# TensorE's order inside attention written out by hand, with one filler matmul between transpositions

## The chip, the cores and the metric

The program runs on one core of a Trainium2 chip, in one launch. The metric is the device time of one execution in microseconds; a comparison of two kernels is made on the same chip, in rounds. All figures of this document are microseconds unless they are marked ns.

## The reference

The reference computes two blocks, one behind the other, on 512 positions of width 1024 (and 256 context positions in the second block). Everything is float32. Cut to what matters here:

```python
# block 1
h = rmsnorm(x) * (1 + scale1) + shift1
qa, ka, va, qb, kb, vb, ga, gb = split(h @ w_in)
ya = mixture_of_dilations(qa, ka, va)      # 8 heads of 64: softmax(q k^T + bias + mask) v
yb = neighbourhood_attention_2d(qb, kb, vb) # 8 heads of 64, window 8 x 16 on a grid of 64 columns
x += gate1 * ((sigmoid(ga) * (ya @ w_a) + sigmoid(gb) * (yb @ w_b)) @ w_out)
x += gate2 * (conv-gated feed forward of x)
# block 2, two layers; every layer has three attentions over latent and context positions
for l in range(2):
    y0 = mla(...)    # 8 heads, q and k of 96 columns, v of 128, dense
    y1 = diff(...)   # 8 heads, p0 - lambda * p1 of two score maps, v of 128, dense
    y2 = swa(...)    # 16 query heads, 4 key heads of 64, window 128 plus the context, with a sink
    x += gate * ((sum_r sigmoid(gm_r) * ((y_r * silu(z_r)) @ w_branch[r])) @ w_out)
```

## The kernel before

**Numbers.** Every product is made in float32r: an operand is held as a high part and a rest, and a projection runs three matmuls for one (`mm3`, lines 336 to 340). A projection of 128 columns over 1024 inputs and 512 positions (`proj`, line 342) is 8 x 3 matmuls of 512 columns, and 8 x 3 of 256 more where the context is projected too. `v_natural` (line 357) and `v_wide` (line 1124) make the values in 256-column matmuls.

**Attention.** Five phases follow each other in the program: the dilated and the neighbourhood attention of block 1, then MLA, diff and SWA, these three twice (layer 0 with context queries, layer 1 without). Each calls `attend` (line 420) with a list of heads; a head has a preparation (its projections, called the mandatory work) and units. A unit is two blocks of 128 queries of one head, and has two halves. `scores` makes the score matmuls (lines 1159 to 1174; into up to three PSUM banks `s`) and the softmax on VectorE and ScalarE. `values` (line 627) transposes the probabilities in groups of up to four 128x128 blocks into one PSUM bank `t` (line 647), splits each group by a ScalarE copy into `pth` and a VectorE subtraction into `ptl` (lines 381 and 382, called from line 651), and multiplies the parts with the values into the bank `pv` (line 665). The pool has one bank for `t` (line 291), two or three buffers each for `pth` and `ptl`.

**Units by phase.** A unit over latent queries has 12 transpositions in three groups of four in MLA and diff (16 and 16 such units over the two layers, each), 9 in groups of 4, 4 and 1 in SWA (32 and 32), 8 in two groups in the dilated attention (16), 5 in groups of 4 and 1 in the neighbourhood attention (16). A unit over context queries has one group of four. That is 1680 transpositions. Score matmuls of a latent unit: MLA 6 of 512 and 6 of 256 columns; diff two maps of 4 of 512 and 4 of 256 each; SWA 6 of 256 and 2 of 384; dilated 4 of 512; neighbourhood 2 of 256 and 2 of 384.

**Filler.** TensorE gets projections between the steps of a unit: `fill` (line 405) draws steps from queues of generators until a number of ns is used up. The queues are the mandatory work of the next head and `opt`, the gate projections that belong to no head. A step of `proj` is three matmuls.

**Order.** `attend` emits, for each unit, the first two groups of transpositions of the unit before, the scores of this one, filler, the first value matmuls, the third group, and so on. This is only the order in which the program is traced. The compiler's list scheduler orders the instructions of each engine anew, by its own times, and may draw ahead whatever it takes to be ready.

**Late work.** `self.late` holds generators that are stepped behind a unit (diff's normalization: `tok_sum`, line 541, writes the bank `t`, and line 558 reads it).

Of the kernel before, what the change touches and what calls it, by code (L numbers as in the profile page):

```python
# [18 lines left out]
P = 128  # L19
# [3 lines left out]
KD = D // P  # L23
# [255 lines left out]
class Prog:  # L279
    def __init__(self, tc, A, out, stage=None):  # L280
        self.tc, self.nc, self.A, self.out, self.stage = tc, tc.nc, A, out, stage
        self.n = 0
        off, self.U = 0, {}
        for name, w, _ in _units():
            self.U[name] = (off, w)
            off += w * P
        self.lay, self.nvec = _vec_layout()
        self.bg, self.ahead, self.late = [], {}, []
        self.wide, self.turn = False, 0
        self.cur = None  # L290
        self.banks = dict(mm=3, t=1, pv=1, s=3)
        self.lo = self.nc.vector
        self.spare = 0


# [39 lines left out]

    def mm3(self, ps, wh, wl, xh, xl, first, last):
        mm = self.nc.tensor.matmul
        mm(ps, wh, xh, start=first, stop=False)  # L338
        mm(ps, wl, xh, start=False, stop=False)  # L339
        mm(ps, wh, xl, start=False, stop=last)  # L340

    def proj(self, name, x, evac, kn=KD, m=P, ctx=False, k0=0, off=0, back=False, ranges=None):

        wt = self.w(name) if isinstance(name, str) else name
        for c0, n in ranges or ((0, S), (S, C))[:2 if ctx else 1][::-1 if back else 1]:
            ps = self.ps("mm")[:m, :n]
            cs = slice(c0, c0 + n)
            for k in range(kn):
                wh, wl = wt.cols(off + k * m, m)
                xh, xl = x[k0 + k] if isinstance(x[k0 + k], tuple) else (x[k0 + k][:, 0], x[k0 + k][:, 1])  # L350
                self.mm3(ps, wh, wl, xh[:, cs], xl[:, cs], k == 0, k == kn - 1)
                if k < kn - 1:
                    yield 3 * n * 0.424
            evac(ps, cs)
            yield 3 * n * 0.424

# [48 lines left out]
    def fill(self, ns, *queues):  # L405


        while ns > 0:
            if self.cur is None:
                q = next((q for q in queues if q and (not isinstance(q[0], tuple) or q[0][0]())), None)  # L410
                if q is None:
                    return
                g = q.pop(0)
                self.cur = g[1] if isinstance(g, tuple) else g
            try:
                ns -= next(self.cur)
            except StopIteration:
                self.cur = None

    def attend(self, heads, opt, opt_ns):  # L420


        nu = sum(len(h[2]) for h in heads)
        pend = None
        for i, (_, _, units) in enumerate(heads):
            mand = heads[i + 1][0]() if i + 1 < len(heads) else []
            mns = heads[i + 1][1] if i + 1 < len(heads) else 0
            for s_, v_ in units:

                vals = pend() if pend else iter(())  # L430
                next(vals, None)
                s_()
                left = mns / len(units) + opt_ns / nu
                ns = left * 0.5
                self.fill(ns, mand, opt)
                for _ in vals:
                    left -= ns
                    self.fill(min(ns, left), mand, opt)
                pend = v_
                self.fill(left - ns, mand, opt)  # L440
                self.tick(1)
                late, self.late = self.late, []
                for g in late:
                    if next(g, 0) is None:
                        self.late.append(g)
            self.finish(mand)
        for _ in pend():
            self.fill(2000, opt)
        while self.late:
            self.late = [g for g in self.late if next(g, 0) is None]  # L450
            self.fill(4000, opt)

    def finish(self, queue):

        while queue:
            self.fill(1, queue)
        self.fill(1e9)

# [168 lines left out]
    def values(self, pv, pp, chunks, stat):  # L627
# [25 lines left out]

        for grp in grps[:2]:
            turn(grp)
        yield
        for i, grp in enumerate(grps):
# [9 lines left out]
            if i + 2 < len(grps):  # L667
                turn(grps[i + 2])
            if i < len(grps) - 1:
                yield  # L670

# [94 lines left out]
    def neighbours(self, h, opt, opt_ns):  # L766

        nc = self.nc
# [6 lines left out]
        def prep(hd):  # L775
# [21 lines left out]
            def ev_v(ps, cs):  # L797
                vt = self.st()
                nc.scalar.activation(own(vt), fwd(ps), AF.Copy)
                for c in range(2):  # L800
                    tp = self.ps("t")
                    for i in range(2):
                        nc.tensor.transpose(tp[:, i * P:i * P + P], vt[:, (2 * c + i) * P:(2 * c + i) * P + P], self.ident)
                    self.v_pairs(va[c], tp[:, :256])

# [51 lines left out]
    def mixer1(self):  # L857
# [5 lines left out]
        with ExitStack() as es:  # L863
# [79 lines left out]
            y = []  # L943
            for f in (lambda: self.dilated(h, line, opt, 42000), lambda: self.neighbours(h, opt, 42000)):
                for yy in f():
# [42 lines left out]
    def ffn(self, x, xq, rbs, h, xd, x_close):  # L988
# [4 lines left out]
        with ExitStack() as es:  # L993
# [21 lines left out]
            def by_halves(nm, ev):  # L1015

                wt, ps = self.w(nm), self.ps("mm")
                for i, (c0, n_) in enumerate(HALVES):
                    cs = slice(c0, c0 + n_)
                    for k in range(KD):  # L1020
                        self.mm3(ps[:, cs], *wt.cols(k * P, P), h[k][:, 0, cs], h[k][:, 1, cs], i == 0 and k == 0,
                                 i == 1 and k == KD - 1)
                        yield 1
# [247 lines left out]
    def mla(self, l, h, ctx):  # L1271
# [60 lines left out]
        def prep(j):  # L1332
            g, e = j // 2, j % 2
            gens = []
            if e == 0:
# [3 lines left out]
                gens.append(self.proj(f"uk{l}_{g}", kvn, ev_k, kn=2, ctx=True))  # L1339
                st["v", g] = [self.page() for _ in range(2)]  # L1340
                gens.append(self.v_wide(f"ux{l}_{g}", kvn, st["v", g], 2))
            q = st["q", j] = self.page()
            ys.append(self.f3())

            def ev_q(ps, cs):
                a = self.st()[:, :ps.shape[-1]]
                if cs.start == 0:
# [4 lines left out]

            gens.append(self.proj(f"uq{l}_{j}", qn, ev_q, kn=3, ctx=ctx))
            if e:

                nc.gpsimd.tensor_copy(kt[1][64:], krp[64:])
            return gens

        def unit(j, q0, lt):
# [11 lines left out]
            def values():  # L1371
# [4 lines left out]
                if q0 in (256, S):  # L1376
# [6 lines left out]

        heads = [(lambda j=j: prep(j), (8900 if j % 2 else 8900), [unit(j, *q) for q in self.qpairs(ctx)])
                 for j in range(KD)]
        self.run_pairs(heads[0][0]())
        yield
# [37 lines left out]
    def diff(self, l, h, ctx):  # L1425
# [33 lines left out]
        def unit(j, q0, lt):  # L1459
# [287 lines left out]
```

## Time and profile before

| | us |
|---|---|
| median of 3 runs | 3565.99 (3561.65 to 3569.0) |
| the profiled execution | 3569.2 |
| its span | 3567.4 |
| TensorE busy | 3436.9 (96%) |
| TensorE's weight loads busy | 2936.5 (82%) |
| VectorE busy | 2352.8 (66%) |
| ScalarE busy | 1808.6 (51%) |

A matmul's record is longer than its place in the stream, since matmuls are pipelined: neighbouring records overlap. What one costs is read from the distance of two starts in the timeline, not from its mean duration. The granted clock is 0.99 over the span. The attention phases lie, from the span's start, at about 84 to 377 (block 1), 963 to 1246 (MLA, layer 0), 1330 to 1826 (diff), 1856 to 2262 (SWA), 2483 to 2690, 2718 to 3150 and 3190 to 3476 (the same three in layer 1).

### The profile page before, as it was taken

The page shows a single profiled execution, that of the slowest core. Times are in us where ns is not written, and L with a number is a line of the kernel's source. Part 1 is how long each engine was busy: PE and PEld are TensorE (multiplying, and loading weights), DVE is VectorE, ACT ScalarE, POOL GpSimd, SP SyncE. Part 2 cuts the span into 40 slices and gives each one's busy share as a digit, 9 for nine tenths or more (in the row PEclk, how much of TensorE's full clock was granted, in tenths as well). Part 3 has the DMA queues.
Part 4 walks back from the last instruction along what each step waited for, and adds up shares of the span by engine and source line. Part 5 has one row for each costly group of instructions (what it writes and reads, how often), then busy time and mean ns, then how long its engine had stood idle before and what let it go on. Part 6 is the DMA issues. An engine that isn't in the chain of part 4 may idle for free. (4 is left out here: it accounts for less than half of the span.)

```text
span 3567.4 us, 54501 instructions
## 1 busy us (share of the span) xinstructions
PE 3436.9 (96%) x19696; PEld 2936.5 (82%) x19696; DVE 2352.8 (66%) x4957; ACT 1808.6 (51%) x4162; POOL 450.2 (13%) x320
## 2 busy tenths in 40 slices
PE   6999999998999999999999999999999999999998
PEld 4777778776888898889888888888888888887777
DVE  7867678876445446567745677655564666757885
ACT  3456444422456525445535777425673454537772
POOL 3001046643000100001100001000010001000010
PEclk9999999998999999999999999999999999999999
DMA  6844545564221153323243211433115333262224
GB/s 227 258 155 120 156 151 161 167 206 133 77 60 35 45 156 85 95 67 85 59 147 106 60 50 47 131 106 90 60 49 149 110 92 92 79 177 80 64 69 142
DMA packets 200351, 392.41 MB, mean 110 GB/s; under 512 B 26289, under 2 KB 39857, under 8 KB 200082
## 3 DMA queue, kind: packets, MB, share of 16 engines
q1 hardware_dynamic: 199378, 385.23, 35.9%
q0 software_dynamic: 704, 3.70, 0.3%
q8 instruction: 155, 2.54, 0.3%
q14 instruction: 114, 0.93, 0.1%
HBM read 302.82 MB, written 38.83 MB: 96 GB/s over the span
## 5 line engine op out<-in xcount | busy, mean ns | idle before, releaser
L338 PE MATMUL mm<-h,whi 128*128 128x512 f32 (+2 forms) x2764 | 1001.9, 363 | 4.7 <-ACT h L601 4.1
L339 PE MATMUL mm<-h,wlo 128*128 128x512 f32 (+2 forms) x2764 | 999.3, 362 | 5.7 <-POOL wlo L275 2.9
L340 PE MATMUL mm<-h,whi 128*128 128x512 f32 (+2 forms) x2764 | 997.0, 361 | 0.1
L274 ACT ACTIVATE whi<-wraw 128x512 fp32r<-128x512 f32 (+1 forms) x763 | 470.5, 622 | 570.1 <-PE mm L340 333.3
L275 DVE TENSOR_TENSOR wlo<-wraw,whi 128x512 fp32r<-128x512 f32 (+1 forms) x627 | 440.8, 708 | 306.7 <-ACT whi L274 302.2
L339 PEld LDWEIGHTS mm<-h,wlo 128*128 128x128 f32 (+1 forms) x2764 | 526.1, 190 | 70.6 <-POOL wlo L275 4.0
L338 PEld LDWEIGHTS mm<-h,whi 128*128 128x128 f32 (+1 forms) x2764 | 526.1, 190 | 69.5 <-ACT h L601 5.0
L340 PEld LDWEIGHTS mm<-h,whi 128*128 128x128 f32 (+1 forms) x2764 | 526.0, 190 | 67.3 <-DVE h L602 0.3
L382 DVE TENSOR_TENSOR ptl<-t,pth 128x512 fp32r<-128x512 f32 (+1 forms) x480 | 298.0, 621 | 160.9 <-ACT pth L381 156.4
L381 ACT ACTIVATE pth<-t 128x512 fp32r<-128x512 f32 (+1 forms) x480 | 260.3, 542 | 221.9 <-PE t L647 217.8
L647 PE MATMUL t<-ident,p 128*128 128x128 f32 x1680 | 287.5, 280 | 30.1 <-DVE ptl L382 19.8
L647 PEld LDWEIGHTS t<-ident,p 128*128 128x128 f32 x1680 | 195.4, 141 | 96.6 <-DVE ptl L382 43.9
L275 POOL TENSOR_TENSOR wlo<-wraw,whi 128x512 fp32r<-128x512 f32 (+1 forms) x136 | 223.2, 1658 | 271.2 <-ACT whi L274 171.1
L338 PE MATMUL mm<-hl,whi 128*128 128x512 f32 (+1 forms) x680 | 242.1, 356 | 6.3 <-ACT hl L381 5.3
L339 PE MATMUL mm<-hl,wlo 128*128 128x512 f32 (+1 forms) x680 | 240.4, 354 | 0.0
L665 PE MATMUL pv<-pth,hl 128*128 128x256 f32 (+1 forms) x1184 | 224.4, 292 | 6.0 <-ACT pth L381 4.7
L1403 POOL TENSOR_TENSOR st<-st,tab 128x512 f32<-128x512 f32 x52 | 76.0, 1462 | 1197.4 <-DMA st<-st 854.0
L665 PEld LDWEIGHTS pv<-pth,hl 128*128 128x128 f32 x1184 | 178.8, 190 | 48.7 <-ACT pth L381 34.2
L1231 POOL TENSOR_TENSOR f<-f,st 128x512 f32<-128x512 f32 x72 | 86.3, 1199 | 784.0 <-DVE st L1230 608.5
L340 PE MATMUL mm<-f,whi 128*128 128x512 f32 (+1 forms) x504 | 178.0, 355 | 0.0
L1199 ACT ACTIVATE p<-s,m 128x512 f32<-128x512 f32 x192 | 132.1, 688 | 90.5 <-DVE m L1194 88.7
L665 PE MATMUL pv<-ptl,hl 128*128 128x256 f32 (+1 forms) x768 | 169.3, 295 | 1.6 <-DVE ptl L382 1.5
(265 smaller groups left out, 6369.7 us busy)
## 6 DMA issues: line engine op xcount, KB each, us to landing
wraw<-in_wst SPq DMA_DIRECT2D x734, 256.0 KB, 2.7
mraw<-in_w_mod SPq DMA_DIRECT2D x48, 512.0 KB, 4.1
hl<-hl SPq DMA_DIRECT2D x128, 192.0 KB, 3.0
mraw<-in_w_ada SPq DMA_DIRECT2D x36, 512.0 KB, 4.6
tg<-st SPq DMA_DIRECT2D x64, 256.0 KB, 2.0
st<-st SPq DMA_DIRECT2D x208, 64.0 KB, 2.0
p<-tg SPq DMA_DIRECT2D x40, 256.0 KB, 2.9
p<-tg SPq DMA_DIRECT2D x24, 384.0 KB, 3.7
```

What stands on the lines that cost most here:

```text
L274: nc.scalar.activation(hi[:, :n], raw[:, :n], AF.Copy)
L275: p.lo.tensor_tensor(lo[:, :n], raw[:, :n], hi[:, :n].bitcast(F32), op=ALU.subtract)
L338: mm(ps, wh, xh, start=first, stop=False)
L339: mm(ps, wl, xh, start=False, stop=False)
L340: mm(ps, wh, xl, start=False, stop=last)
L381: nc.scalar.activation(dst_h, src, AF.Copy)
L382: nc.vector.tensor_tensor(dst_l, src, dst_h.bitcast(F32), op=ALU.subtract)
L647: self.nc.tensor.transpose(tp[:, o + i * P:o + i * P + P], pp[t][:, cols[i]:cols[i] + P], self.ident)
L665: mm(dst, sv, x_[:, o:o + w], start=first, stop=last)
L1199: nc.scalar.activation(p[:, 0:S], a[t], AF.Exp, bias=m[:, 2 + t:3 + t], accum_out=m[:, 4 + t:5 + t])
L1231: nc.gpsimd.tensor_tensor(ys[j][:, cs], ys[j][:, cs], th, op=ALU.mult)
L1403: nc.gpsimd.tensor_tensor(a, a, tab[0], op=ALU.mult)
```

## The change

- `attend` runs inside `tc.manual_schedule(engines={PE})`: inside it TensorE issues its instructions in the order in which the program emits them. The other engines stay with the scheduler.
- `mm3` becomes a generator, and inside attention (`self.fine`) a step of `proj` is one matmul.
- `values` says where it stands: "turn" between two transpositions of a group, "scores" behind the first group, "copies" behind the second, "rest" behind each further step. `unit` puts one filler step at each "turn", the scores at "scores", a quarter of the unit's remaining filler at "copies" and 0.15 of it at each "rest", and what is left at the end.
- `self.left` is a balance of filler that is carried from unit to unit; `fill` returns what it used, `finish` what it had to add.
- MLA's preparation comes in three parts: k, then q as the last of the head's filler, then the values of a pair of heads behind the first unit of the head that needs them. The budgets of filler change (8900 to 1950 or 3900, and 2930 or 1950 ns; 42000 to 36000 in block 1).
- diff's scores are issued one map at a time, the second behind "copies"; the neighbourhood's transpositions of the values (line 803) become late work.

```diff
     def mm3(self, ps, wh, wl, xh, xl, first, last):
         mm(ps, wh, xh, start=first, stop=False)
+        yield
         mm(ps, wl, xh, start=False, stop=False)
+        yield
         mm(ps, wh, xl, start=False, stop=last)
...
-                self.mm3(ps, wh, wl, xh[:, cs], xl[:, cs], k == 0, k == kn - 1)
+                left = 3
+                for _ in self.mm3(ps, wh, wl, xh[:, cs], xl[:, cs], k == 0, k == kn - 1):
+                    if self.fine and left > 1:
+                        left -= 1
+                        yield n * 0.424
...
+        with self.tc.manual_schedule(engines={mybir.EngineType.PE}):
+            for i, (_, _, units) in enumerate(heads):
+                mand = heads[i + 1][0]() if i + 1 < len(heads) else []
+                mand, last, late = mand if isinstance(mand, tuple) else (mand, [], [])
+                mns = heads[i + 1][1] if i + 1 < len(heads) else 0
+                for u, (s_, v_) in enumerate(units):
+                    self.left += mns / len(units) + opt_ns / nu
+                    self.unit(s_, pend, (mand, opt), (behind, last if u == len(units) - 1 else [], mand, opt))
+                    self.left -= self.finish(behind)
+                    pend = v_
+                    self.tick(1)
+                    todo, self.late = self.late, []
+                    for g in todo:
+                        if next(g, 0) is None:
+                            self.late.append(g)
+                self.left -= self.finish(mand) + self.finish(last)
+                behind = late
...
+    def unit(self, s_, pend, queues, after):
+        def put(ns, queues):
+            self.left -= self.fill(min(ns, self.left), *queues)
+        rest = share = None
+        for what in (pend() if pend else iter(())):
+            if what == "turn":
+                self.left -= self.fill(1, *queues)
+            elif what == "scores":
+                rest = s_()
+                share = self.left
+                if rest is not None:
+                    next(rest)
+            else:
+                put((0.25 if what == "copies" else 0.15) * share, queues)
+                if what == "copies" and rest is not None:
+                    next(rest, None)
+                    rest = None
...
+        put(self.left, after)
...
                 for i, t in enumerate(ts):
+                    if o or i:
+                        yield "turn"
                     self.nc.tensor.transpose(...)
...
-        for grp in grps[:2]:
-            turn(grp)
-        yield
+        yield from turn(grps[0])
+        yield "scores"
+        for grp in grps[1:2]:
+            yield from turn(grp)
+        yield "copies"
...
-            gens.append(self.proj(f"uq{l}_{j}", qn, ev_q, kn=3, ctx=ctx))
...
-            return gens
+            return gens, [self.proj(f"uq{l}_{j}", qn, ev_q, kn=3, ctx=ctx)], late
...
-                (p0, s0, e), (p1, s1, f) = [self.exps(*self.scores(mp, (q, k), lt, q0)) for mp in range(2)]
+                p0, s0, e = self.exps(*self.scores(0, (q, k), lt, q0))
+                yield
+                p1, s1, f = self.exps(*self.scores(1, (q, k), lt, q0))
```

## Rows read from the trace of the kernel before

**Rows 1.** The page's first part: busy time, share of the span, instructions.
```profile
PE 3436.9 (96%) x19696; PEld 2936.5 (82%) x19696; DVE 2352.8 (66%) x4957; ACT 1808.6 (51%) x4162; POOL 450.2 (13%) x320
```

**Rows 2.** Attention's stretches: length, busy PE, PEld, DVE, ACT, POOL (instructions), clock; last, sum.
```profile
3190.00:3476.00 286.00, 277.71 (x1544) 221.71 (x1542) 224.01 (x602) 207.89 (x565) 20.27 (x15) 1.00 0.28 82
sum 2403.00, PE 2351.77 PEld 2022.96 DVE 1586.44 ACT 1383.62 POOL 185.55; mean PE 335.97 PEld 288.99 DVE 226.63 ACT 197.66 POOL 26.51
```

**Rows 3.** TensorE's groups by shape, SWA of layer 1, 3230 to 3476.
```profile
L339 PE MATMUL mm<-h,wlo 128*128 128x512 f32 x166 | 67.1, 404 | 0.0
...
L647 PE MATMUL t<-ident,p 128*128 128x128 f32 x270 | 49.8, 283 | 5.5 <-DVE ptl L382 4.1 <-ACT p L611 1.0
L665 PE MATMUL pv<-ptl,hl 128*128 128x256 f32 x120 | 27.9, 313 | 0.0
...
L1174 PE MATMUL s<-hl,hl 128*128 128x256 f32 x86 | 20.0, 288 | 0.0
...
L1174 PE MATMUL s<-hl,hl 128*128 128x384 f32 x28 | 9.7, 346 | 0.0
...
L665 PE MATMUL pv<-ptl,hl 128*128 128x128 f32 x30 | 7.3, 244 | 0.7 <-DVE ptl L382 0.6
L338 PE MATMUL mm<-hl,whi 128*128 128x512 f32 x18 | 7.2, 401 | 0.0
```

**Rows 4.** Timeline of SWA, layer 1: start, length, engine, line, operation, count.
```profile
3331.47 0.60 PE L647 MATMUL t<-ident,p 128*128 128x128 f32 x4
3331.83 0.48 PE L665 MATMUL pv<-ptl,hl 128*128 128x256 f32 x2
3332.15 0.40 PE L339 MATMUL mm<-h,wlo 128*128 128x512 f32 x1
...
3332.38 0.40 PE L340 MATMUL mm<-h,whi 128*128 128x512 f32 x1
3332.62 0.69 PE L1172 MATMUL s<-hl,hl 128*128 128x256 f32 x4
3332.80 0.69 DVE L382 TENSOR_TENSOR ptl<-t,pth 128x512 fp32r<-128x512 f32 x1 [0.46 <-ACT pth L381]
3333.14 0.41 PE L665 MATMUL pv<-pth,hl 128*128 128x256 f32 x2
3333.93 0.27 PE L647 MATMUL t<-ident,p 128*128 128x128 f32 x1
3333.95 0.48 PE L665 MATMUL pv<-ptl,hl 128*128 128x256 f32 x2
3334.27 0.40 PE L338 MATMUL mm<-h,whi 128*128 128x512 f32 x1
```

**Rows 5.** The same timeline, one unit earlier: a slower split.
```profile
3321.31 0.48 PE L665 MATMUL pv<-ptl,hl 128*128 128x256 f32 x2
...
3323.40 0.69 DVE L382 TENSOR_TENSOR ptl<-t,pth 128x512 fp32r<-128x512 f32 x1
...
3324.14 0.33 PE L647 MATMUL t<-ident,p 128*128 128x128 f32 x1 [0.34 <-DVE ptl L382]
...
3324.22 0.36 PE L665 MATMUL pv<-pth,hl 128*128 128x256 f32 x1
```

**Rows 6.** TensorE's waits over the whole span: total, times, longest.
```profile
PE t L647 <- DVE ptl L382: 19.8, 29, 1.6
```

**Rows 7.** Timeline of MLA, layer 1: the end of a q projection and its evacuation.
```profile
2635.86 0.39 PE L340 MATMUL mm<-hl,whi 128*128 128x512 f32 x1
...
2636.36 0.69 DVE L1348 TENSOR_TENSOR st<-mm,tab 128x512 f32<-128x512 f32 x1 [0.53 <-PE mm L340]
...
2638.11 0.64 ACT L381 ACTIVATE hl<-st 128x512 fp32r<-128x512 f32 x1
...
2638.78 0.69 DVE L382 TENSOR_TENSOR hl<-st,hl 128x512 fp32r<-128x512 f32 x1 [0.16 <-ACT hl L381]
```

**Rows 8.** The view of line 558, 2790 to 3150: durations in ns (min/median/max).
```profile
L558 DVE SCALAR_TENSOR_TENSOR rstd<-t,eps x8: 160/161/163, 2818.2 to 3122.9; 128x4 f32<-128x4 f32 x8
```

More of the change, by code (lines that the diff above doesn't have):

```diff
@@ L405, in fill @@
     def fill(self, ns, *queues):
-        while ns > 0:
+        done = 0
+        while ns > done:
             if self.cur is None:
@@ L425, in attend @@
[L425 to L451, printed above, removed]
+        pend, behind = None, []
+        self.fine, self.left = True, 0
+        with self.tc.manual_schedule(engines={mybir.EngineType.PE}):
[15 more added lines that the diff above has]
+                behind = late
+            for what in pend():
+                self.fill(220 if what == "turn" else 1500, opt)
+            while self.late:
+                self.late = [g for g in self.late if next(g, 0) is None]
+                self.fill(4000, opt)
@@ new lines, in attend @@
+        self.fine = False
+    def unit(self, s_, pend, queues, after):
[15 more added lines that the diff above has]
+                    rest = None
+        if share is None:
+            rest = s_()
+            if rest is not None:
+                next(rest)
+                put(0.4 * self.left, after)
+                next(rest, None)
+                rest = None
+        put(self.left, after)
@@ L453, in finish @@
     def finish(self, queue):
-        while queue:
-            self.fill(1, queue)
-        self.fill(1e9)
+        ns = 0
+        while queue or self.cur is not None and self.cur_of is queue:
+            ns += self.fill(1, queue)
+        return ns
     def silu_row(self, name):
@@ L667, in values @@
             if i + 2 < len(grps):
-                turn(grps[i + 2])
+                yield from turn(grps[i + 2])
             if i < len(grps) - 1:
-                yield
+                yield "rest"
     def fold_pair(self, pv, par, y, view=lambda a: a):
@@ L799, in ev_v, with turns @@
                 nc.scalar.activation(own(vt), fwd(ps), AF.Copy)
[L800 to L804, printed above, removed]
+                def turns():
+                    for c in range(2):
+                        tp = self.ps("t")
+                        for i in range(2):
+                            nc.tensor.transpose(tp[:, i * P:i * P + P], vt[:, (2 * c + i) * P:(2 * c + i) * P + P],
+                                                self.ident)
+                        self.v_pairs(va[c], tp[:, :256])
+                    yield
+                if self.fine:
+                    self.late.append(turns())
+                else:
+                    self.run_all([turns()])
             return [self.proj(f"qn{g}", h, ev_q),
@@ L943, in mixer1 @@
             y = []
[L944 removed]
+            for f in (lambda: self.dilated(h, line, opt, 36000), lambda: self.neighbours(h, opt, 36000)):
                 for yy in f():
@@ L1339, in prep, with values @@
                 gens.append(self.proj(f"uk{l}_{g}", kvn, ev_k, kn=2, ctx=True))
-                st["v", g] = [self.page() for _ in range(2)]
-                gens.append(self.v_wide(f"ux{l}_{g}", kvn, st["v", g], 2))
-            q = st["q", j] = self.page()
+                def values():
+                    st["v", g] = [self.page() for _ in range(2)]
+                    yield from self.v_wide(f"ux{l}_{g}", kvn, st["v", g], 2)
+                late.append(values())
             ys.append(self.f3())
             def ev_q(ps, cs):
+                if cs.start == 0:
+                    st["q", j] = self.page()
+                q = st["q", j]
                 a = self.st()[:, :ps.shape[-1]]
```

25 lines of the change are left out of this document (14 added, 11 removed).

## The prediction

> **What bounds the kernel now.** I read the page's first part, then the stretches of attention, then one stretch's matmuls by shape, then a timeline inside it. TensorE is busy for 96% of the span, VectorE for 66% [rows 1]: TensorE is the bound, and the question is what it loses. In the seven stretches of attention it is busy for 2351.8 of 2403 us [rows 2], so 51 us are plain idle time. That understates the loss, because a record overlaps the next one. The price of a matmul in the stream is the distance of two starts: 0.23 for 512 columns (3332.15 to 3332.38) and 0.52 for three of 256 and one of 384 (3332.62 to 3333.14), so 0.12 and about 0.17 [rows 4]. Four transpositions take 0.36 until the next matmul starts, and the two behind them take 0.32 where 0.24 is their price, so four cost 0.44, or 0.11 each [rows 4].
>
> With these prices I count one stretch, SWA of layer 1: 549 matmuls of 512 columns (three groups of 165 or 166, the 18, and three alike that are not shown, 34 together), 412 of 256 (two groups of 120, two of 86), 56 of 384, 60 of 128 at 0.11, and 270 transpositions [rows 3]: 126.3 + 49.4 + 9.5 + 6.6 + 29.7 = 221.5 of 246 us. So 24.5 are lost there, while the records leave 8.3 uncovered in a stretch that holds this one [rows 2]: three times as much. At that ratio attention loses about 51 x 3 = 153 us, 4% of the time. This is all that a better order can win; the rest is work that the change keeps.
>
> Where the loss sits: the longest wait of TensorE in attention is that of a transposition for the subtraction that empties its bank, 19.8 us in 29 waits [rows 6]. Much of the rest is small: a weight load that has waited starts late, and the matmul behind that transposition starts 0.08 after it (3324.14 to 3324.22) [rows 5] instead of 0.02 (3333.93 to 3333.95) [rows 4], some 0.05 more.
>
> **The change part by part.** *The order.* The timeline shows how the scheduler works now: four transpositions, then value matmuls, filler and scores for 2.1 us, and only then the next transposition [rows 4]. The bank `t` is the reason: the copy and the subtraction (0.69) must both have read it. There the subtraction starts at 3332.80 and ends at 3333.49, which is 1.66 after the first matmul behind the group started; a release takes 0.05 more (3324.09 to 3324.14) [rows 5], so 1.71. Where VectorE and ScalarE have other work first it is 2.83 [rows 5]. The new program puts only the scores between the first and the second group, and no filler: "turn" stands between transpositions alone. TensorE can no longer draw anything ahead, so behind the second group's first transposition queue all scores' successors, fillers and value matmuls, and nobody else can use the engine.
>
> So the slot between the groups has a fixed cover: the scores, and 0.08 for the first matmul behind a transposition. MLA: 6 x 0.23 + 6 x 0.12 + 0.08 = 2.18. diff, one map: 4 x 0.23 + 4 x 0.12 + 0.08 = 1.48. SWA: 6 x 0.12 + 2 x 0.17 + 0.08 = 1.14. Dilated: 4 x 0.23 + 0.08 = 1.00. Neighbourhood: 2 x 0.12 + 2 x 0.17 + 0.08 = 0.66.
>
> Against a bank that comes free 1.71 behind: MLA nothing, diff 0.23 x 32 units = 7, SWA 0.57 x 64 = 36, dilated 0.71 x 16 = 11, neighbourhood 1.05 x 16 = 17: 71 us. At 2.83: 21 + 43 + 108 + 29 + 35 = 236. I take 1.80, near the low row: in the new order the softmax that is to be transposed is done when the group is, and the next has not begun, so less stands before the copy than in [rows 5]. That gives 0.32 x 32 + 0.66 x 64 + 0.80 x 16 + 1.14 x 16 = 10 + 42 + 13 + 18 = **83 us of new waits**.
>
> *The second slot of SWA* (second to third group) holds a quarter of the remaining filler and the first value matmuls. A unit has 3900 ns of filler by its budgets, three fillers are gone at the "turns", a quarter of 3250 is four matmuls: 4 x 0.23 + 4 x 0.12 + 0.08 = 1.48. Against 1.71 that lacks 0.23, against 1.80 it lacks 0.32, against 2.83 it lacks 1.35: 15, 20 or 86 us in 64 units. I take 20. In MLA and diff this slot has over 2.5 us of filler and values or scores; nothing.
>
> *MLA's q as the last filler of a head.* Nothing stands behind it but four transpositions with three fillers (0.44 + 0.69 = 1.13), in layer 0 also its own context part (9 x 0.12 = 1.07). Then the scores want q. Now the evacuation takes from the last matmul's start at 2635.86 to 2639.47, that is 3.6, of which 1.06 is a wait for ScalarE (2637.05 to 2638.11) [rows 7]; without it 2.5. The rest of q is first read by the third score matmul, 0.46 later. Layer 1 lacks 2.5 - 1.13 - 0.46 = 0.9 to 2.0 in seven heads, layer 0 nothing to 0.9: 6 to 20 us. I take 12. The parts themselves are the same matmuls at other places, and the DMAs of their weights are issued by the same loader three buffers ahead: nothing.
>
> *diff's normalization* writes bank `t` behind a unit and must be read by line 558 (0.16, [rows 8]) before the next transposition: 0.27 for the tail of a matmul's record [rows 4], 0.16 and the release make 0.5 with no cover, 24 times: 12 us; 4 if the probabilities come later anyway, 29 if VectorE is in another operation of 0.69. I take 8.
>
> *The filler behind each transposition.* The timeline has both orders [rows 4]: four in a row cost 0.11 each; the single one at 3333.93 costs 0.02 until its successor starts, and the successor and the one behind it take 0.32 for 0.24, so 0.10. A single one saves nothing, and some 1200 of 1680 get a filler behind them: zero, between -12 (0.01 each) and +20 (a third of them with the 0.05 of a late weight load).
> The Trainium skill ("TensorE: Matmul & The Clock Gate", Part 2: What happens when you issue a matmul) says that the engine pulls a weight load ahead of matmuls in flight, so that the next weights load while this matmul runs; by it a filler would hide a transposition's load. By that rule the transposition would be left with its streaming; the trace has the same price with and without a matmul beside it, so that the sum by the rows has nothing here.
>
> *What is removed.* The present loss of about 153. All that the records leave idle, 51, is the low end; the high end is 140, since some of it stands in any order (the first matmul behind a transposition, the spread of starts). I take 100, two thirds: a transposition's wait and the late weight load behind it both go where fillers are placed well. diff's second map behind "copies" and the carried balance belong to this: they spread filler, they remove no matmul.
>
> *The clock* is granted at 1.00 in the last stretch [rows 2], its upper level of 2.4 GHz, though waits of up to 1.6 occur [rows 6]. Waits of the size forecast here leave it there: nothing.
>
> **Sum:** 83 + 20 + 12 + 8 + 0 - 100 = +23 us against the profiled execution of 3569.2, so 3592. That execution lies 3.2 above the median of the runs shown; as a median I forecast **3589**, 0.6% slower. With all ends at their best, 71 + 15 + 6 + 4 - 12 - 140 = -56, so 3510; with the new waits at 2.83 far more than 3700, which would need every split to be as slow as the slowest shown.
>
> **The rivals.** *Faster, because the old loss goes whole.* The splits land at 1.71 and 130 of the 153 go: 71 + 15 + 6 + 4 - 130 = -34, 3532. For it: the loss is there, and the new order is regular. Against it: the new waits in SWA alone take half of that back, since one bank and 1.14 of cover cannot meet 1.71. It decides where the removed part exceeds the new waits, about 123 at my values. Chance 0.25.
> *Faster, because a filler hides the transposition's weights.* 1200 x 0.08 = 96 less: 3493. It is the skill's rule above as a mechanism; for it only that a late load does cost something now, against it the 0.10 of the single one [rows 4]. Chance 0.10.
> *Slower by much: the split is queued.* With ScalarE and VectorE busy for 208 and 224 of 286 in SWA [rows 2], the subtraction falls behind the score reductions that the same scores have just fed to VectorE; the bank comes free at 2.3. Then the first slot costs 4 + 26 + 74 + 21 + 26 = 151 instead of 83: 3657. It decides from about 2.0 on. Chance 0.15.
> *The change hardly shows.* The scheduler's present order is near the program's (groups of four, scores, filler), so that what it loses by the bank it loses in either, and the sum is nothing: 3566. Chance 0.08.
> The forecast itself has 0.42, of which 0.02 fall within 0.2%.
>
> **How the numbers follow.** Faster by over 0.2%: 0.25 + 0.10 = 0.35. Within 0.2% (7 us, about what a measurement of this kernel can tell from no change): 0.08 + 0.02 = 0.10. Slower: 0.40 + 0.15 = 0.55. The range is 3512 to 3668: it holds the forecast, the first rival and the queued split, and leaves out most of the hidden weights and the far end of the waits. Cases of both signs hold much of the chance; the forecast's own range is 3570 to 3625.
>
> **What would show it.** Right: TensorE's wait of the transpositions for the subtraction of line 382 grows from 19.8 to 60 or more, with some 60 to 130 waits, most of them in SWA and block 1 and hardly one in MLA; those stretches get longer (SWA of layer 1 by 10 us) and MLA's and diff's do not. The transpositions stand singly between matmuls, and one with its filler takes 0.33 to 0.34. Wrong: if such a pair takes 0.25 to 0.28, the fillers do hide the loads; if the first transposition of a second group starts without a wait 1.1 behind the first group, the bank is not what I take it for; if SWA gets shorter, the loss removed is larger than 100.

## The result and the profile after

| | before | after |
|---|---|---|
| median in the comparison | 3567.5 | 3958.4 (3947.7 to 3964.7) |
| ratio | | 1.109, interval 1.107 to 1.111 |
| span of the profiled execution | 3567.4 | 3951.8 |
| TensorE busy | 3436.9 | 3537.6 |

The change makes the kernel 11% slower. The page of the kernel after, its first part, the row of the granted clock and the group of the transpositions (busy, mean ns | idle time just before them and what ended most of it):

```profile
span 3951.8 us, 54535 instructions
...
PE 3537.6 (90%) x19696; PEld 2998.5 (76%) x19696; DVE 2380.2 (60%) x4957; ACT 1818.2 (46%) x4162; POOL 455.0 (12%) x320
...
PEclk8899999998999999999899998999999999999999
...
L691 PE MATMUL t<-ident,p 128*128 128x128 f32 x1680 | 459.1, 293 | 256.1 <-DVE ptl L390 153.9
```

The same group in the kernel before:

```profile
L647 PE MATMUL t<-ident,p 128*128 128x128 f32 x1680 | 287.5, 280 | 30.1 <-DVE ptl L382 19.8 <-DVE p L613 3.6 <-ACT p L611 2.7
```

TensorE executes the same 19696 matmuls as in [rows 1], and VectorE and ScalarE are busy for at most 1.2% longer. But TensorE is idle for 3951.8 - 3537.6 = 414 us, before for 130, and the records of its matmuls cover 101 more. Of the idle time 256 stands just before transpositions, before 30. Its waits in the whole span (total, times, longest), beside the one of [rows 6]:

```profile
PE t L691 <- DVE ptl L390: 153.9, 144, 5.8
PE t L691 <- ACT p L653: 60.8, 30, 4.8
PE s L1229 <- ACT p L1256: 27.8, 33, 3.6
...
PE t L691 <- DVE rstd L600: 12.0, 21, 1.9
...
PE t L691 <- DVE m L1629: 10.3, 7, 1.5
PE t L691 <- DVE p L1534: 10.1, 9, 2.5
...
PE s L1223 <- ACT hl L389: 5.0, 6, 1.4
```

Line 691 is the transposition, 390 the subtraction that empties its bank, 653 the scaling of the probabilities, 1534 the step that joins diff's two maps, 600 diff's normalization, 1629 a step of SWA's softmax, 1229 a score matmul that waits until line 1256, the exponential, has read a bank. The 10.3 under line 1629 belong to the split too: all seven of these waits stand in front of a unit's second group (one of them is shown below), and the subtraction ends just before the transposition starts, there at 2341.40 before 2341.54.

**Where the time went, by phases.** I cut both traces at the last transposition of each phase and counted in each stretch its length, TensorE's idle time, and the time at the lower granted clock (0.50). "Free" is experiment 1, the same program with the order left to the scheduler. "Work" is TensorE's matmuls times their price in a clean stream at full clock (0.227 for 512 columns, 0.119 for 256, 0.175 for 384, 0.11 for a transposition or 128).

| phase | length before | free | after | work before | after | idle before | free | after | lower clock before | after |
|---|---|---|---|---|---|---|---|---|---|---|
| to dilated | 269 | 240 | 266 | 206 | 166 | 38 | 37 | 63 | 20 | 44 |
| neighbourhood | 112 | 144 | 176 | 103 | 140 | 2 | 4 | 24 | 0 | 10 |
| MLA 0 | 845 | 849 | 880 | 778 | 785 | 33 | 30 | 51 | 34 | 58 |
| diff 0 | 562 | 563 | 616 | 543 | 530 | 6 | 8 | 55 | 0 | 31 |
| SWA 0 | 471 | 467 | 582 | 431 | 439 | 15 | 12 | 87 | 3 | 79 |
| MLA 1 | 413 | 417 | 465 | 392 | 397 | 7 | 7 | 42 | 7 | 34 |
| diff 1 | 447 | 438 | 463 | 427 | 415 | 7 | 5 | 27 | 10 | 14 |
| SWA 1 | 353 | 351 | 408 | 322 | 329 | 11 | 10 | 53 | 0 | 14 |
| rest | 96 | 96 | 96 | 81 | 82 | 12 | 12 | 12 | 12 | 8 |
| sum | 3567 | 3565 | 3952 | 3282 | 3282 | 130 | 125 | 414 | 87 | 291 |

The work is the same, 3282. What lies above it is 286 before and 670 after. Idle time takes 284 of the 384 more. At half the clock half of the busy time is lost. Of the 291 us at the lower clock TensorE stands idle for 51, of the 87 before for 18, so that the clock takes (240 - 69) / 2 = 86. What is neither, 286 - 130 - 35 = 121 before, is 670 - 414 - 120 = 136 after: that loss did not shrink, it grew by 15. Two of the stretches of after, SWA's (length, busy PE, PEld, DVE, ACT, POOL, clock, DMA share, GB/s):

```profile
1938.00:2520.00 582.00, 494.90 (x2917) 427.13 (x2918) 325.17 (x807) 296.63 (x784) 32.52 (x26) 0.93 0.23 67
...
3448.00:3856.00 408.00, 355.26 (x1961) 291.74 (x1960) 264.50 (x670) 232.96 (x610) 29.05 (x19) 0.98 0.29 85
```

**What the waits look like.** The timeline of after in SWA, layer 0 (start, length, engine, line, operation): a unit's softmax, and the first transposition of its values.

```profile
2348.57 0.69 PE L1231 MATMUL s<-hl,hl 128*128 128x256 f32 x4
...
2350.58 0.41 DVE L1623 CUSTOM_DVE_ANT_0 p<-s,wmask 128x256 f32<-128x256 f32 x1
...
2353.22 0.45 ACT L1633 ACTIVATE p<-s,m 128x256 f32<-128x256 f32 x1
...
2353.55 0.39 PE L342 MATMUL mm<-h,wlo 128*128 128x512 f32 x1
...
2355.80 0.91 ACT L653 ACTIVATE p<-p,m 128x256 f32<-128x256 f32 x2 [0.49 <-DVE m L1642]
...
2356.36 0.33 PE L691 MATMUL t<-ident,p 128*128 128x128 f32 x1 [2.42 <-ACT p L653]
```

From the end of the scores (2349.26) to the first probabilities that a transposition may read (2356.36) it is 7.1 us, a chain that goes from VectorE to ScalarE, back, and to ScalarE again. The written order has 4.7 us of work for it, until 2353.94; then TensorE stands, though the next instruction behind the transposition is a filler that waits for nothing.

The other kind, MLA of layer 1, the third group of a unit. A row of ScalarE's begins with ACT; line 389 is the copy out of the bank:

```profile
2769.76 0.27 PE L691 MATMUL t<-ident,p 128*128 128x128 f32 x1
...
2769.79 0.72 PE L712 MATMUL pv<-pth,hl 128*128 128x256 f32 x4
...
2770.34 0.40 PE L712 MATMUL pv<-ptl,hl 128*128 128x256 f32 x2
...
2770.45 0.67 ACT L1256 ACTIVATE p<-s,m 128x512 f32<-128x512 f32 x1
...
2773.43 1.76 ACT L653 ACTIVATE p<-p,m 128x768 f32<-128x768 f32 x2
2775.21 0.60 ACT L389 ACTIVATE pth<-t 128x512 fp32r<-128x512 f32 x1
2775.84 0.69 DVE L390 TENSOR_TENSOR ptl<-t,pth 128x512 fp32r<-128x512 f32 x1 [1.71 <-ACT pth L389]
2776.59 0.47 PE L691 MATMUL t<-ident,p 128*128 128x128 f32 x1 [5.84 <-DVE ptl L390]
```

The group before it was transposed at 2770.03. ScalarE then did the next unit's whole exponentials and scaling (2770.45 to 2775.19) and only then the copy. The order of ScalarE and VectorE is the scheduler's, and no run changed it. The slot held six value matmuls and no filler; TensorE waited 5.84.

The third kind, the second group of a unit in SWA, layer 0, where the unit that follows is one of context queries:

```profile
2339.33 0.27 PE L691 MATMUL t<-ident,p 128*128 128x128 f32 x1
...
2339.35 0.48 PE L1229 MATMUL s<-hl,hl 128*128 128x256 f32 x2
...
2339.67 0.40 PE L1231 MATMUL s<-hl,hl 128*128 128x256 f32 x2
2340.11 0.69 DVE L1626 TENSOR_REDUCE m<-s 128x2 f32<-128x512 f32 x1 [1.87 <-PE s L1231]
2340.72 0.68 DVE L390 TENSOR_TENSOR ptl<-t,pth 128x512 fp32r<-128x512 f32 x1
...
2341.54 0.30 PE L691 MATMUL t<-ident,p 128*128 128x128 f32 x1 [1.47 <-DVE m L1629]
```

The slot between the groups holds the scores of the unit that follows, and these are four matmuls of 256 here, 0.48 in all, not the eight of a latent unit. VectorE does the maximum of these scores before the subtraction.

**The clock.** Granted clock around the wait that ended at 2356.36 (same columns as above; the clock is the one with two decimals behind POOL's):

```profile
2353.50:2356.30 2.80, 0.44 (x2) 0.02 (x1) 1.05 (x5) 2.31 (x10) 0.00 (x0) 1.00 0.00 0
2356.80:2360.20 3.40, 3.40 (x14) 3.04 (x14) 1.02 (x2) 0.60 (x1) 0.00 (x0) 0.50 0.00 0
2360.30:2366.20 5.90, 5.79 (x42) 5.00 (x41) 3.59 (x15) 4.64 (x15) 0.00 (x0) 1.00 0.18 44
```

Behind the wait of 2.42 the clock falls from its upper level (2.4 GHz) to the lower (1.2 GHz) for 3.4 us, and rises again with no idle time in between. The changed kernel has 56 such stretches, the one before 13. All but one of the 56 begin close behind a wait or several, or inside one, with 1.1 to 4.9 us of idle time just ahead.

### The profile page after: what moved, and what is told of

Its sections match the earlier page's. It is cut to its first block, busy times and chain, and to the rows that moved or that the text cites. A ratio compares the mean times of both kernels' runs of the same rounds, so it can differ in the third digit from the quotient of the medians.

```text
span 3951.8 us, 54535 instructions
## 1 busy us (share of the span) xinstructions
PE 3537.6 (90%) x19696; PEld 2998.5 (76%) x19696; DVE 2380.2 (60%) x4957; ACT 1818.2 (46%) x4162; POOL 455.0 (12%) x320
## 5 line engine op out<-in xcount | busy, mean ns | idle before, releaser
L340 PE MATMUL mm<-h,whi 128*128 128x512 f32 (+2 forms) x2764 | 1039.6, 376 | 5.4 <-ACT h L643 4.5
L342 PE MATMUL mm<-h,wlo 128*128 128x512 f32 (+2 forms) x2764 | 1037.1, 375 | 4.1 <-DVE wlo L275 2.5
L344 PE MATMUL mm<-h,whi 128*128 128x512 f32 (+2 forms) x2764 | 1032.8, 374 | 0.1
L691 PE MATMUL t<-ident,p 128*128 128x128 f32 x1680 | 459.1, 293 | 256.1 <-DVE ptl L390 153.9
L340 PEld LDWEIGHTS mm<-h,whi 128*128 128x128 f32 (+1 forms) x2764 | 538.2, 195 | 81.4 <-ACT h L643 5.4
L342 PEld LDWEIGHTS mm<-h,wlo 128*128 128x128 f32 (+1 forms) x2764 | 536.0, 194 | 78.4 <-issue 3.8
L344 PEld LDWEIGHTS mm<-h,whi 128*128 128x128 f32 (+1 forms) x2764 | 533.5, 193 | 74.5 <-issue 2.4
L691 PEld LDWEIGHTS t<-ident,p 128*128 128x128 f32 x1680 | 236.3, 144 | 333.2 <-DVE ptl L390 147.0
L712 PE MATMUL pv<-pth,hl 128*128 128x256 f32 (+1 forms) x1184 | 218.0, 291 | 11.7 <-ACT pth L389 11.2
L712 PEld LDWEIGHTS pv<-pth,hl 128*128 128x128 f32 x1184 | 188.0, 197 | 37.6 <-ACT pth L389 19.6
L1229 PE MATMUL s<-hl,hl 128*128 128x256 f32 (+2 forms) x640 | 170.1, 366 | 35.2 <-ACT p L1256 27.8
```

Of the source, the lines that this page charges most:

```text
L712: mm(dst, sv, x_[:, o:o + w], start=first, stop=last)
L1229: mm(ps, q[:, par, q_], k[:, par, k_], start=st[0], stop=False)
```

## The experiments

Twelve kernels were run, each beside the kernel before on the same chip. All times are medians. My theory from the traces above: the work is unchanged and the price of a matmul too; what costs is the written order, which has too little between a producer and its consumer. The rivals were that the steps of the order (single transpositions, one bank) cost by themselves, and that the other parts (balance, MLA's parts, finer filler) do.

**1. The order left to the scheduler, all else as in the change.**

```diff
-        with self.tc.manual_schedule(engines={mybir.EngineType.PE}):
+        with ExitStack():
```

> The whole change without the fixed order of TensorE; the program's own order, fillers, balance and MLA's parts stay. Theory (the fixed order makes the loss: TensorE stands at waits it could have passed by, and its clock falls for that): idle time of TensorE back to about 130 us, granted clock back to 0.985 or more, 3550 to 3600 us. Rival (the finer mix of transpositions and fillers or the new budgets cost by themselves): over 3700 us.

Measured: 3567.1, ratio 0.999 (0.998 to 1.000). The whole loss is the fixed order's; the rest of the change together is worth nothing that can be told. Its wait for the split, and two of its stretches, those of the two SWA phases:

```profile
PE t L691 <- DVE ptl L390: 8.8, 18, 1.4
```

```profile
1796.00:2263.00 467.00, 455.35 (x2857) 390.49 (x2856) 317.35 (x801) 290.20 (x782) 31.99 (x26) 1.00 0.27 81
...
3118.00:3469.00 351.00, 340.60 (x1916) 276.86 (x1914) 258.29 (x666) 229.28 (x606) 25.90 (x18) 1.00 0.33 96
```

The scheduler's order is fixed too, when the program is compiled. It is only a better one: 144 waits for the split become 18.

**2. Fixed order, no filler between the transpositions of a group.**

```diff
                     if o or i:
-                        yield "turn"
+                    if False:
+                        yield "turn"
```

> The change with the fixed order, but no filler between the transpositions of a group. Theory (a filler between transpositions neither saves nor costs TensorE's time): within 1% of the change, 3920 to 4000 us. Rival (the filler hides the weight load of a transposition, some 0.08 us of each of 1200): 4030 us or more. Rival (the filler makes the splits late): under 3900 us.

Measured: 3922.1, ratio 1.099 (1.097 to 1.101). 36 of 391 come back; the single transpositions are not the cause. A part of the 36 is filler that now stands in the slots: the wait for the split falls from 153.9 to 93.9.

**3. Fixed order, two banks for transpositions (and two instead of three for projections).**

```diff
-dict(mm=3, t=1, pv=1, s=3)
+dict(mm=2, t=2, pv=1, s=3)
```

> The change with two PSUM banks for transpositions and two instead of three for projections. Theory (the second group's first transposition waits for the one bank, some 110 us of idle time in the trace of the change, and the clock falls with it): the wait for line 390 falls from 154 us to under 40, 3790 to 3860 us. Rival (the waits move to the next thing that the fixed order meets, the softmax of the first group): the sum of idle time falls by less than half of that, 3900 us or more.

Measured: 3926.6, ratio 1.100 (1.098 to 1.102), far above what my theory gave it. TensorE's waits:

```profile
PE t L691 <- ACT p L653: 97.5, 57, 4.8
PE s L1229 <- ACT p L1256: 43.1, 40, 3.8
PE pv L712 <- ACT pth L389: 31.8, 29, 4.3
PE pv L712 <- DVE ptl L390: 27.4, 37, 1.3
PE mm L340 <- DVE hl L390: 24.0, 11, 4.1
```

The wait of the transposition for the split is gone from the list. Its time isn't: the next transposition waits for its own softmax (60.8 before, 97.5 now), the value matmuls for the split that the transposition used to wait for (11.2 + 6.1 before, 59.2 now), and projections wait for their bank. The chain stays as long as it was, and TensorE meets it one instruction later.

**4. Fixed order, filler also between the first and the second group.**

```diff
                 if rest is not None:
                     next(rest)
+                put(0.25 * share, queues)
```

> The change with a quarter of a unit's remaining filler between the scores and the second group of transpositions, which leaves less at the unit's end. Theory (the slot behind the scores is too short): the same waits go as with two banks, 3800 to 3880 us. Rival (the filler is missed behind the unit, where the softmax is awaited): no more than 40 us are won, 3915 us or more.

Measured: 3915.0, ratio 1.097 (1.095 to 1.099). The same picture:

```profile
PE t L692 <- ACT p L654: 83.5, 69, 4.8
PE t L692 <- DVE ptl L390: 72.9, 56, 6.0
```

The split's wait falls by 81 and the softmax's grows by 23 (numbers of lines are one higher here); the time falls by 43. The filler is a fixed amount, and what covers one slot is missing in the next.

**5. Fixed order, values two units behind the scores in SWA and block 1.**

```diff
-                    self.unit(s_, pend, (mand, opt), ...)
-                    pend = v_
+                    self.unit(s_, pend.pop(0) if len(pend) == deep else None, (mand, opt), ...)
+                    pend.append(v_)
```

> The change, but in SWA and in block 1 the transpositions and value matmuls come two units behind their scores instead of one, so that the softmax has a whole unit more. Theory (what is left of the loss there is the first transposition of a unit that waits for its softmax): in SWA the waits for lines 653 and 1629, 59 us in the trace of the change, fall under 10, the waits for line 390 stay, and the time is 3880 to 3920 us with the clock that comes back. Rival (a wait taken away is met again at the next instruction in order, since VectorE and ScalarE are late as a whole): 3930 us or more.

Measured: 3923.3, ratio 1.099 (1.097 to 1.102). Waits:

```profile
PE t L691 <- DVE ptl L390: 174.3, 152, 5.8
...
PE t L691 <- ACT p L653: 14.0, 7, 4.8
```

Now the softmax has a unit's time and its wait falls from 60.8 to 14.0, and the split's grows by 20.

**6. Three together: two banks, values two units behind, and 0.35 instead of 0.25 of the filler behind the second group.**

> Three cures together under the fixed order: two banks for transpositions (two for projections), the values two units behind in SWA and block 1, and 0.35 instead of 0.25 of the remaining filler in front of diff's second map. Theory (the loss is the sum of waits with separate causes): the cures add up to 130 us or more, 3830 us or less. Rival (every order that is fixed by hand meets the same lateness of VectorE and ScalarE): under 90 us together, 3870 us or more.

Measured: 3804.1, ratio 1.066 (1.064 to 1.068). Alone the first two bring 32 and 35, all three bring 154. The third was not run alone, so that how much is its own stays open. TensorE's idle time falls from 414 to 292, the lower clock stays at 288 us.

**7. Fixed order, with five more matmuls of 512 columns ahead of each SWA unit's first transposition** (400 matmuls whose result nobody reads, 92 us of work by their price).

> The change with five matmuls of 512 columns more (1.15 us, their result unused) in front of the first transposition of each of SWA's 80 units, 92 us of work. Theory (TensorE's clock falls because the engine waits, and each wait costs twice): in SWA of layer 0 the granted clock rises from 0.93 to 0.98 or more, and the time grows by less than 40 us. Rival (the clock falls by the mix of short matmuls and transpositions): the clock stays at 0.93 there and the time grows by 60 us or more.

Measured: 4025.2, ratio 1.128 (1.126 to 1.130): 67 for 92 us of added work, so 25 came back, 16 of them idle time (414 to 398). The softmax's wait falls from 60.8 to 38.9, the clock of SWA's layer 0 rises from 0.93 to 0.96 (at the lower clock for 51 us instead of 79). Neither side is shown clean: 1.15 us of cover is half of a wait like the 2.42 above, and most units have none there (24 of these waits in the change stand in SWA's 80 units).

**8. The kernel before with two banks for transpositions and two for projections.**

> The kernel before, its order left to the scheduler, with two banks for transpositions and two for projections. Theory (the scheduler fills the wait for the bank already, 19.8 us are left of it): 3540 to 3565 us. Rival (two banks for projections are too few): 3580 us or more.

Measured: 3619.1, ratio 1.014 (1.012 to 1.016). In the scheduler's order the third projection bank is worth 52 us more than a second one for transpositions. In the fixed order this price was not measured by itself, but projections wait more there too (24.0 for line 390 in experiment 3, 4.3 in the change), so that experiments 3 and 6 probably understate what the second transposition bank brings.

**9. The free order without fillers between transpositions** (experiment 2's edit with experiment 1's).

> The changed kernel with TensorE's order left to the scheduler, and besides no filler step between the transpositions of a group, as in the kernel before. Theory (the loss lies in the written order alone, and the scheduler arranges TensorE by its own times whatever the program says): the time of the free version with fillers, 3567, within 10 us: 3557 to 3577. Rival (the order in which the program is traced still leads the scheduler, and in the free version a loss by the single transpositions cancels a gain from the better spread filler): without them the time falls by the 36 us that they cost in the fixed order (3958 to 3922), so 3530 to 3545.

Measured: 3559.3, ratio 0.9974 (0.9964 to 0.9984). This is the one version that is faster than before, by 0.26%. Single transpositions cost some 8 us in this order (3567.1 to 3559.3), not 36; the rest of experiment 2's gain I put down to the filler's place, which no run tells apart by itself.

**10. Fixed order, the cures without a second bank** (experiments 4 and 5, and 0.35 behind the second group).

> The fixed order with the cures that take no PSUM bank from the projections, all at once: a quarter of the unit's filler also behind the scores (before the second group), 0.35 of it instead of 0.25 behind the second group, and values two units behind the scores in SWA and block 1. Banks as in the change. Theory (each wait is a chain of softmax or split with too little work beside it, cures add up only when given together, and the third projection bank is worth some 50 us by itself): at or below the 3804 of the version with two banks, 3760 to 3820, with TensorE idle under 280 and under 200 us at the lower clock. Rival (the second bank for transpositions is what made the combination work; with one bank the waits for the split come back): about the sum of the single cures, 3958 - 43 - 35 = 3880, with the wait of the transpositions for the subtraction still over 60 us.

Measured: 3868.2, ratio 1.084 (1.083 to 1.086): the rival's 3880, not my 3760 to 3820. Its largest wait:

```profile
PE t L692 <- DVE ptl L390: 87.7, 69, 5.8
```

With one bank the split's wait stays. That the second bank is what made experiment 6 work, in spite of its price, is likely but not shown: the two runs differ in the filler behind the scores too. In experiment 6 the split is waited for by the value matmuls (42.2 and 40.6) and by hardly a transposition.

**11. The program of 10 with the order left to the scheduler.**

> The same program as the one with all cures and no bank change (a quarter behind the scores, 0.35 behind the second group, values two units behind), but with TensorE's order left to the scheduler. Theory (the scheduler finds its own places and has already covered the chains; there are 125 us of idle left, little of it in attention): 3555 to 3580, no difference from before. Rival (the traced order leads the scheduler, and values two units behind give it more that is ready): 10 to 40 us faster, 3527 to 3557.

Measured: 3566.4, ratio 0.999 (0.998 to 1.000). The scheduler makes the same time of three different programs (experiments 1, 9, 11, within 8 us); 10 and 11 differ in nothing but who orders TensorE, and lie 302 us apart.

**12. The order fixed in the two SWA phases alone.**

```diff
-        with self.tc.manual_schedule(engines={mybir.EngineType.PE}):
+        with self.tc.manual_schedule(engines={mybir.EngineType.PE}) if fixed else ExitStack():
```

> The changed kernel with TensorE's order fixed in the two SWA phases alone; in block 1, MLA and diff it is left to the scheduler. Between the free version and the change the phases differ by 115 (SWA layer 0), 56 (SWA layer 1), and 214 in the others together. Theory (each phase's loss is local: its own chains, its own waits and the clock that they pull down): SWA keeps its loss and the others lose theirs, so 3567 + 115 + 56 = 3738, within 20: 3718 to 3758, SWA layer 0 at 570 to 590 and MLA and diff within 10 of the free version's. Rival (the loss is shared between phases by what one leaves the next: filler drawn too early, weights that come late, the balance): the SWA phases alone cost much less than 171, under 3690, or the free phases beside them get longer by over 10 each.

Measured: 3700.0, ratio 1.036 (1.034 to 1.039). The stretches, SWA 0, SWA 1, MLA 0 and diff 0:

```profile
1797.00:2357.00 560.00, 476.55 (x2858) 411.10 (x2856) 322.39 (x802) 296.29 (x783) 31.50 (x26) 0.95 0.23 68
3214.00:3605.00 391.00, 340.15 (x1917) 278.60 (x1916) 262.42 (x666) 231.42 (x607) 27.23 (x18) 1.00 0.30 87
382.00:1234.00 852.00, 823.17 (x4298) 693.14 (x4297) 569.55 (x975) 397.67 (x787) 247.77 (x154) 0.97 0.39 120
1234.00:1797.00 563.00, 555.26 (x3590) 496.98 (x3589) 348.00 (x757) 251.49 (x625) 40.18 (x32) 1.00 0.32 89
```

The loss is local: no phase outside SWA differs from the free version by more than 3 us. The sum is 38 under my theory, for three reasons. In the change the SWA phases also held 20 us of filler that other phases had not used (work 439.0 and 328.5, free 428.6 and 318.8); that part was no loss. The lower clock took 61 and 0 us instead of 79 and 14, in which TensorE was busy for 57 instead of 83, worth 13. And the idle time is 6 less (83 and 51, in the change 87 and 53). Layer 1 shows an order's cost without the clock: 40 us longer than the free version's 351, at a granted clock of 1.00, with 51 - 10 = 41 us more idle.

## Why the prediction failed, point by point

I forecast 3589 (3512 to 3668); it is 3958. The sign was right, the size by far not. Three steps of the sum failed: the new waits, priced at 123 because only the slots inside the values were counted, with covers that many of them did not have (the idle time grew by 284); the 100 to be removed from the old loss (nothing was removed); and the clock, set to nothing (it took 86).

- **TensorE is the bound, the work stays:** right. The matmuls are the same, 3282 us by their prices.
- **New waits in the first slot, 83:** right in kind, and for the slots that it describes in size too; but it describes too few. From TensorE's idle time ahead of the first transposition of each second group I get 113: SWA 50 (forecast 42), diff 27 (10), dilated 17 (13), neighbourhood 13 (18), MLA 5 (0). I gave every slot the scores of a latent unit. What stands in it is the scores of the unit that follows, and behind the second latent unit of a layer-0 head that is a context unit: four matmuls of 256 in SWA and diff, 0.48, six in MLA, 0.71. These 31 slots hold 46 of the 113 (30 in SWA, 11 in diff, 5 in MLA), all others 67. Of the time at which the bank comes free, my 1.80 was near in SWA's full slots and block 1 (the subtraction ends 1.75 to 1.9 behind the group on average), not in diff (2.1 to 2.6) and in SWA's short slots (2.6). There VectorE and ScalarE take the next unit's softmax or a projection's evacuation in between, which is the mechanism of the rival of the queued split; its 151 was too much.
- **SWA's second slot, 20:** 28, inside its range.
- **MLA and diff nothing in the slots that have over 2 us of cover:** failed in MLA. The wait for the split stands there 20 times with 31 us. In 16 of the 20 the slot held six score or value matmuls and no filler, 0.71: the filler that I counted on was used up, or the scores were a context unit's. The three longest (5.84, 5.12 and 5.12) have the next unit's exponentials and scaling ahead of the copy on ScalarE, as shown above. I compared a cover that was often not there with a latency from a free queue. In diff's third groups, with 4.8 and 5.8 us of cover on average in the two layers, no transposition waits: right.
- **MLA's q, 12, and diff's normalization, 8:** 5.0 and 12.0; right.
- **A filler behind a transposition, 0:** right. At full clock a pair takes 0.34 (2342.26 to 2342.60):

```profile
2342.26 0.27 PE L691 MATMUL t<-ident,p 128*128 128x128 f32 x1
2342.28 0.48 PE L342 MATMUL mm<-h,wlo 128*128 128x512 f32 x1
2342.60 0.27 PE L691 MATMUL t<-ident,p 128*128 128x128 f32 x1
```

  That is 0.11 + 0.23: the filler hides none of the transposition's price, and the rival with the hidden weights falls. In the free order it costs 8 us (experiment 9).
- **What was not in the sum at all:** a unit's first transposition waits for its own softmax (60.8 and 10.1 in the list of waits), and diff's second map, mostly, for the exponentials that hold its banks (27.8). I had asked of each slot inside the values what covers it, and not of the two slots at their borders, which the same fixed order makes as rigid.
- **Removed, 100:** failed. I called two thirds of the old loss removable by a better order. The loss that is neither idle time nor clock was 121 and is 136, and the plain idle time did not go but tripled. The free version has nearly all of it too (125 idle), and the fastest order tried here, experiment 9, took 8 us out.
- **The clock, nothing:** failed, by 86. I read the clock of the last stretch beside a longest wait of 1.6 from the whole span (it stood in block 1); the new waits are longer, up to 5.84, and come many times.

So +384 is 284 of waits, 86 of clock and some 15 of the loss that is neither; my sum had 123 of waits, no clock, and 100 back. The terms that I priced hold 113 + 28 + 5 + 12 = 158 of the waits; the borders hold 60.8 + 10.1 + 27.8 = 99 and MLA's third groups 25.5. (These are whole waits; the old order had some of the kind too, 30 in front of transpositions.)

What stays open: which waits pull the clock down and which don't. It doesn't go with the idle time: experiment 6 has 122 us less idle time than the change and 288 us at the lower clock against 291, and SWA's layer 1 has 51 us idle without any in experiment 12. There the longest wait of layer 1 is 2.1 and all others are 1.6 or less; in layer 0, with 61 us at the lower clock, they go up to 3.3. No run separates the length of a wait from how often waits come.

## What to carry to other kernels

An engine's order written by hand needs, for every wait in it, the length of the chain behind that wait with all that stands ahead of it on the other engines, not the latency of its last step, and the cover that really stands in the slot: here the scores in it were those of the unit that follows, and the filler could be used up. A slot left uncovered moves its wait to the next instruction when one cure is given alone (experiments 3 to 5), so that cures are judged together. Before fixing an order, run the same program with the scheduler's: here that one kept the engine busy for 96%, and there was little to win and much to lose. Waits can also pull down TensorE's clock; here that added 30% to what they cost.

## What the runs showed of the hardware

- With waits of 1.1 to 4.9 us just ahead the granted clock fell to 0.50 for 3.4 to 14 us at a time, 55 times in the execution after (a 56th time without one). A pair of a transposition and a 512-column matmul then takes 0.64 (2371.80 to 2372.44) instead of 0.34:

```profile
2371.80 0.41 PE L691 MATMUL t<-ident,p 128*128 128x128 f32 x1
...
2372.44 0.41 PE L691 MATMUL t<-ident,p 128*128 128x128 f32 x1
```

- Two PSUM banks each for projections and transpositions, instead of three and one, cost 1.4% in the scheduler's order (experiment 8).
- TensorE's records are no measure of its work: the same 19696 matmuls have 3436.9 us of busy time before and 3537.6 after, and by the distances of their starts at full clock they are 3282 in both.
